# Two-layer diffusion backbone on one core: low parts, Y sums and squares of the projections pinned behind the VectorE work issued before them while a norm chain runs

## The chip, the core and the metric

The kernel runs on one core of one Trainium2 chip. TensorE (PE) multiplies, VectorE (DVE) and ScalarE (ACT) do the elementwise work, SyncE (SP) issues nearly all transfers, GpSimd (POOL) is unused. The metric is the device time of one execution in microseconds (us), the median of the runs; lower is better. One execution was also profiled, and all views are of that one. The trace gives the TensorE clock as a granted share: 1.0 is 2.4 GHz and 0.5 is 1.2 GHz.

## The reference, cut to what matters

There are 640 tokens (512 latent, 128 context) of width 1024, and two layers. Each layer is a feed-forward block, a token mixer (differential attention in layer 0, a gated linear recurrence, HGRN2, in layer 1) and another feed-forward block: six sub-layers in a row. Each of the six has a norm before and a norm after:

```python
def ada_pre(x, mod, j, g):
    return rmsnorm(x, g) * (1 + scale) + shift
def ada_post(x, y, mod, j, g, res_w):
    return x + res_w * gate * rmsnorm(y, g)
def ffn_sublayer(x, mod, j, g_pre, g_post, w_in, w_out):
    return ada_post(x, swiglu(ada_pre(x, mod, j, g_pre), w_in, w_out), mod, j, g_post, 0.5)
```

So between two sub-layers every token passes: sum of squares of the output Y, reciprocal root, X plus the scaled Y, sum of squares of X, reciprocal root, scaled X, which is the input H of the next projection.

## The kernel before, in words

Activations lie transposed: 128 features on the partitions, tokens along the row, eight blocks of 128 features. The 640 tokens are two groups of 320, g=0 and g=1.

**Projections.** A projection is a list of jobs; a job multiplies one 128-column unit of weights with H (or G, the hidden activations) for one group or both. Weights and activations are each split into a high and a low part: `convert` has ScalarE make the high part of a unit (L360) and puts the low part's subtraction on VectorE (L362) on a list, which `flush_lo` empties at the next unit or shortly after. Per feature block a job issues two matmuls with the high part (L452) and one with the low part (L457). The unit of a job is converted about three jobs ahead of it. Raw weights come through four buffers. The last projection of a sub-layer adds its parts into Y (L1132, VectorE, or a copy by ScalarE for a first part), and a square of Y (ScalarE, L555) is added to a sum `acc` (L556, VectorE). Four PSUM banks are taken in turn.

**Links.** `link` joins two sub-layers. The last eight jobs of the old one come once for g=0 and then for g=1. When g=0 is done, its norm chain (`chain_gen`) starts in the background beside the g=1 jobs; when g=1 is done, the second chain starts beside the first g=0 jobs of the next sub-layer (eight of a feed-forward block, five of attention, seven of HGRN), and it must be issued whole before that sub-layer's first g=1 job. A chain is, in order: three small matmuls that sum `acc` over partitions (L522), a reciprocal root by Newton steps on VectorE (L529, then L507 to L517), a matmul that spreads it over the partitions (L534), eight blocks of X plus scaled Y (L573, L579) with squares (L556), then again L522, L529 to L517 and L534, and eight blocks of scaled X, of which ScalarE makes the high part of H (L611) and VectorE the low part (L606 before, L619 after it). A step of a chain is issued at fixed places within the jobs (`step_bg`).

**Order.** What stands in the program in this order is the order of issue. A scheduler then fixes the order on each engine at compile time: of the instructions that its model of time holds to be ready, it takes the one issued first. So an instruction issued later can come ahead of one that is not yet ready, if nothing ties them. In the trace, each engine runs the order that was fixed.

The five links are called here A (feed-forward to attention), B (attention to feed-forward), C (feed-forward to feed-forward), D (feed-forward to HGRN) and E (HGRN to feed-forward). c0 and c1 are the chains of the two groups. J0, J1, ... are the first jobs of the sub-layer after a link; for a feed-forward block J0 to J7 are for g=0 and J8 on for g=1, where J8 and J9 use the weights of J6 and J7, and J10 and J11 those of J4 and J5, while J12 on load theirs again.

Of the kernel before, what the change touches and what calls it, by code (L numbers as in the profile page):

```python
# [14 lines left out]
ALU = mybir.AluOpType  # L15
# [203 lines left out]
class Net:  # L219
# [31 lines left out]
    def setup(self):  # L251
        tc, ctx = self.tc, self.ctx
        P = lambda n, b, **k: ctx.enter_context(tc.tile_pool(name=n, bufs=b, **k))
        self.const = P("const", 1)
        self.big = P("big", 1)
        self.rawp = P("rawp", RAW_BUFS)
        self.hlp = P("hlp", 1)
        self.hl = self.hlp.tile([128, 2, QUARTERS * 4, 128], F32R, name="whl")
        self.hl_next = 0
        self.los = []  # L260
        self.np_ = P("nrm", 3)
        self.small = P("small", 2)
        self.aux = P("aux", 2, space=PSUM)
        self.mm = P("mm", 1, space=PSUM)
        self.spill = P("spill", 1, space=bass.MemoryType.DRAM)
        self.lane = 0
        self.in_attn = False
        big = self.big
        self.Y = [big.tile([128, KT, NG], F32, name="Y0"), None]
        self.new_x()  # L270
        self.H = big.tile([128, 2, KT, NTOK], F32R, name="H")
        c = self.const
        self.ident = c.tile([128, 128], F32, name="ident")
        self.sel = c.tile([128, 3, 32], F32, name="sel")
        self.CV = c.tile([128, KT, 2], F32, name="CV")
        self.ones = c.tile([128, 1], F32, name="ones")
        self.MODF = c.tile([128, DEPTH * NMOD * KT, 2], F32, name="MOD")
        self.MOD = self.MODF.rearrange("p (l n) s -> p l n s", l=DEPTH)
        self.NGt = c.tile([128, 96], F32, name="NGt")
        self.BM = c.tile([128, 144], F32, name="BM")  # L280
        self.DT = c.tile([128, 50], F32, name="DT")
        self.PRE = c.tile([128, DEPTH, 3, KT, 2], F32, name="PRE")
        self.POST = c.tile([128, DEPTH, 3, KT, 2], F32, name="POST")
        self.acc = {}
        for g in range(2):
            self.acc[g] = c.tile([128, NG], F32, name=f"acc{g}")
        self.lam = c.tile([128, 1], F32, name="lam")
        self.lb = c.tile([128, 2, 16], F32, name="lb")
        self.again = c.tile([128, 1], F32, name="again")
# [35 lines left out]
    def place(self, u):  # L325
# [11 lines left out]
        u.w = [self.hl[:, r, 4 * a:4 * b, :] for r in range(2)]  # L337
        return True

    def flush_lo(self):  # L340
        for f in self.los:
            f()
        self.los.clear()

    def convert(self, n):
# [279 lines left out]

    def chain_gen(self, l, j, nxt, g, ready):
        ps = self.aux_tile()
        yield from self.post_gen(l, j, g, ps, nxt is not None)
        if nxt is not None:
            yield from self.pre_gen(nxt[0], nxt[1], g, ps, ready)  # L630
        else:
            yield from self.store_gen(g)

    def store_gen(self, g):
        nc = self.nc
        for tb in (0, 1, 2):
            n = min(NG - tb * 128, 128)
            ps = self.aux_tile()
            for kt in range(KT):
                nc.tensor.transpose(  # L640
                    ps[0:n, kt * 128:(kt + 1) * 128], self.X[:, kt, tb * 128:tb * 128 + n], self.ident
                )
            ob = self.fin_p.tile([128, 1024], F32, name="ob", tag="ob", bufs=2)
            nc.scalar.activation(out=ob[0:n, 0:512], in_=ps[0:n, 0:512], func=AF.Copy)
            nc.vector.tensor_copy(ob[0:n, 512:1024], ps[0:n, 512:1024])
            nc.sync.dma_start(out=self.o["y_sample"][0, tb * 128:tb * 128 + n, :], in_=ob[0:n, :])
            yield
# [478 lines left out]
    def y_part(self, f, ps, g, first, last):  # L1126
        nc = self.nc
        y = self.Y[g][:, f, :]
        if first:
            nc.scalar.activation(out=y, in_=ps, func=AF.Copy)  # L1130
        else:
            nc.vector.tensor_tensor(out=y, in0=y, in1=ps, op=ALU.add)  # L1132
        if last:
            while len(self.later) > 1:
                self.later.pop(0)()
            self.later.append(self.square(g, y, f == 0))

    def w_out_jobs(self, w, ready, cut):
        jobs = []
# [588 lines left out]
```

## Time and profile before

| | |
|---|---|
| time, median of 3 runs | 2783.96 us (2780.76 to 2785.59) |
| the profiled execution's own time | 2780.47 us |
| its span in the trace | 2778.7 us |
| mean granted TensorE clock | 0.99 |
| TensorE matmuls busy | 2715.6 us (98%) |
| VectorE busy | 1977.8 us (71%) |
| ScalarE busy | 1307.3 us (47%) |

The span goes from the first to the last instruction; 1.8 us of the execution's time lie outside it. Busy shares are means over stages with different limits. A line number is that of the kernel before.

### The profile page before, as it was taken

The page shows a single profiled execution, that of the slowest core. Times are in us where ns is not written, and L with a number is a line of the kernel's source. Part 1 is how long each engine was busy: PE and PEld are TensorE (multiplying, and loading weights), DVE is VectorE, ACT ScalarE, POOL GpSimd, SP SyncE. Part 2 cuts the span into 40 slices and gives each one's busy share as a digit, 9 for nine tenths or more (in the row PEclk, how much of TensorE's full clock was granted, in tenths as well). Part 3 has the DMA queues.
Part 4 walks back from the last instruction along what each step waited for, and adds up shares of the span by engine and source line. Part 5 has one row for each costly group of instructions (what it writes and reads, how often), then busy time and mean ns, then how long its engine had stood idle before and what let it go on. Part 6 is the DMA issues. An engine that isn't in the chain of part 4 may idle for free.

```text
span 2778.7 us, 47467 instructions
## 1 busy us (share of the span) xinstructions
PE 2715.6 (98%) x18670; PEld 2613.1 (94%) x18670; DVE 1977.8 (71%) x4285; ACT 1307.3 (47%) x2693; POOL 0.2 (0%) x4
## 2 busy tenths in 40 slices
PE   7999999899999999999999999999999999999998
PEld 5999999899998999999999999999999999999997
DVE  6766676887777965667786657687677678867574
ACT  4443444476675553435354434443343345545363
POOL 0000000000000000000000000000000000000000
PEclk9999999999999999999999999999999999999999
DMA  9556224211122456524244442421221222323231
GB/s 305 176 192 198 81 77 145 60 53 54 46 74 75 161 161 201 165 81 145 69 143 132 142 145 77 137 78 35 61 58 50 60 65 93 90 77 90 78 122 54
DMA packets 426077, 299.10 MB, mean 108 GB/s; under 512 B 9051, under 2 KB 386429, under 8 KB 424829
## 3 DMA queue, kind: packets, MB, share of 16 engines
q1 hardware_dynamic: 425344, 295.86, 34.6%
q8 instruction: 147, 2.41, 0.4%
q14 instruction: 78, 0.63, 0.1%
q10 hardware_dynamic: 508, 0.20, 0.0%
HBM read 280.82 MB, written 15.20 MB: 107 GB/s over the span
## 4 chain that ended last, share of the span: by engine, by line
PE 89%; DVE 5%; ACT 4%; DMA 1%; issue 1%; ACTq 0%; DVEq 0%; SPq 0%
PE mmps L484 31%; PE mmps L452 30%; PE mmps L457 15%; PE aux L1564 2%; PE aux L763 2%; PE mmps L1403 1%; DVE whl L362 1%; PE aux L1372 1%; ACT p L1302 1%; PE aux L1373 1%; PE aux L522 1%; PE aux L1601 1%; PE aux L534 1%; ACT whl L360 1%; ACT sq L1635 0%
## 5 line engine op out<-in xcount | busy, mean ns | idle before, releaser
L360 ACT ACTIVATE whl<-wraw 128x512 fp32r<-128x512 f32 (+4 forms) x644 | 464.2, 722 | 661.3 <-PE mmps L452 369.6
L362 DVE TENSOR_TENSOR whl<-wraw,whl 128x512 fp32r<-128x512 f32 (+4 forms) x644 | 515.3, 801 | 207.8 <-ACT whl L360 199.6
L452 PE MATMUL mmps<-H,whl 128*128 128x320 f32 x2624 | 571.5, 317 | 9.3 <-ACT H L611 6.9
L484 PE MATMUL mmps<-H,whl 128*128 128x320 f32 x3456 | 544.1, 309 | 0.1
L484 PEld LDWEIGHTS mmps<-H,whl 128*128 128x128 f32 x3456 | 515.3, 188 | 10.5 <-issue 4.2
L452 PE MATMUL mmps<-G,whl 128*128 128x320 f32 x2448 | 487.7, 311 | 3.8 <-ACT G L1649 1.5
L452 PEld LDWEIGHTS mmps<-H,whl 128*128 128x128 f32 x2624 | 432.5, 191 | 19.5 <-ACT H L611 8.3
L452 PEld LDWEIGHTS mmps<-G,whl 128*128 128x128 f32 x2448 | 391.2, 188 | 13.7 <-issue 5.9
L457 PE MATMUL mmps<-H,whl 128*128 128x320 f32 x1312 | 369.6, 314 | 0.7 <-DVE whl L362 0.7
L484 PE MATMUL mmps<-T,whl 128*128 128x320 f32 x2160 | 352.5, 309 | 0.0
L484 PEld LDWEIGHTS mmps<-T,whl 128*128 128x128 f32 x2160 | 325.4, 188 | 5.0 <-issue 2.5
L457 PE MATMUL mmps<-G,whl 128*128 128x320 f32 x1224 | 304.9, 310 | 0.0
L457 PEld LDWEIGHTS mmps<-H,whl 128*128 128x128 f32 x1312 | 239.1, 191 | 1.1 <-DVE whl L362 1.0
L457 PEld LDWEIGHTS mmps<-G,whl 128*128 128x128 f32 x1224 | 211.4, 188 | 0.0
L452 PE MATMUL mmps<-G,H 128*128 128x320 f32 x880 | 198.7, 312 | 0.1
L1132 DVE TENSOR_TENSOR Y<-Y,mmps 128x320 f32<-128x320 f32 x208 | 94.8, 482 | 127.8 <-PE mmps L457 127.6
L452 PEld LDWEIGHTS mmps<-G,H 128*128 128x128 f32 x880 | 147.8, 189 | 0.3 <-ACT Y L1130 0.3
L457 PE MATMUL mmps<-G,H 128*128 128x320 f32 x440 | 137.3, 312 | 0.0
L452 PE MATMUL mmps<-H,G 128*128 128x320 f32 x448 | 103.5, 312 | 0.0
L997 ACT ACTIVATE sa<-sa 128x320 f32<-128x320 f32 x144 | 67.9, 471 | 66.4 <-DVE sa L1000 65.5
L135 DVE TENSOR_TENSOR s<-wraw 128x512 f32<-128x512 f32 x72 | 49.7, 690 | 69.0 <-DMA wraw<-in_ffn_w_in 68.9
L556 DVE TENSOR_TENSOR acc<-acc,sq 128x320 f32<-128x320 f32 x168 | 80.1, 485 | 22.1 <-ACT sq L555 21.2
(260 smaller groups left out, 3572.5 us busy)
## 6 DMA issues: line engine op xcount, KB each, us to landing
wraw<-in_ffn_w_in SPq DMA_DIRECT2D x192, 512.0 KB, 4.3
wmod<-in_w_mod SPq DMA_DIRECT2D x66, 1024.0 KB, 7.1
wraw<-in_hgrn_w_in SPq DMA_DIRECT2D x40, 512.0 KB, 3.9
wraw<-in_ffn_w_out SPq DMA_DIRECT2D x32, 448.0 KB, 3.7
wraw<-in_ffn_w_out SPq DMA_DIRECT2D x32, 384.0 KB, 3.3
wraw<-in_attn_w_in SPq DMA_DIRECT2D x24, 512.0 KB, 3.8
xs<-X SPq DMA_DIRECT2D x4, 2560.0 KB, 12.8
wraw<-in_ffn_w_out SPq DMA_DIRECT2D x32, 320.0 KB, 3.2
```

Of the source, the lines that this page charges most:

```text
L135: V.tensor_tensor(out=z, in0=a[:, lo], in1=b[:, lo], op=ALU.subtract)
L360: nc.scalar.activation(out=u.w[0][:, 0:nk, :], in_=src, func=AF.Copy)
L362: self.los.append(lambda: nc.vector.tensor_tensor(out=u.w[1][:, 0:nk, :], in0=src, in1=u.w[0][:, 0:nk, :].bitcast(F32), op=ALU.subtract))
L452: nc.tensor.matmul(out=ps[g][:, 0:NG], lhsT=w[0][:, a, :], rhs=rhs[:, r, b, g * NG:(g + 1) * NG], start=(i == 0 and r == 0), stop=False,)
L457: nc.tensor.matmul(out=ps[g][:, 0:NG], lhsT=w[1][:, a, :], rhs=rhs[:, 0, b, g * NG:(g + 1) * NG], start=False, stop=(i == last),)
L484: nc.tensor.matmul(out=ps[:, 0:NG], lhsT=w[a][:, k, :], rhs=j.operand(r, k), start=(j.first and k == 0 and n == 0), stop=(k == 3 and n == ...
L522: self.nc.tensor.matmul(out=ps[:, c0 + n:c0 + n + 1], lhsT=acc[:, b0:b0 + 128], rhs=self.ones, start=True, stop=True,)
L556: return lambda: nc.vector.tensor_tensor(out=acc, in0=acc, in1=sq, op=ALU.add)
L763: self.nc.tensor.matmul(out=ps[g * 32:(g + 1) * 32, 0:512], lhsT=CS[:, k, 30 - 2 * i:62 - 2 * i], rhs=ts[half][:, g, :], start=first and h ...
L997: A.activation(out=e[name], in_=e[name], func=AF.Silu)
L1132: nc.vector.tensor_tensor(out=y, in0=y, in1=ps, op=ALU.add)
L1564: nc.tensor.matmul(out=ps[:, c * 128:(c + 1) * 128], lhsT=km[:, c * 128:(c + 1) * 128], rhs=self.view(Q2, c * 128, dims), start=True, stop ...
```

## The change

A counter `chains` holds how many chains are being issued. While it is above zero, the low parts, the later adds into Y, and the adds of Y's squares are each tied to the VectorE instruction issued just before them: `keep_in_program_order` records that the instruction may not stand ahead of that one in VectorE's order. It is a tie of order alone, without a semaphore. Instructions that are issued later are not tied, and neither are the chains' own instructions, the product of the gated hidden activations (L969, L972), or low parts that are issued after a chain has ended. No instruction is added or removed.

```diff
@@ setup
         self.los = []
+        self.chains = 0
@@
+    def behind(self, ins):
+
+        if self.chains:
+            self.tc.keep_in_program_order(ins)
+
     def flush_lo(self):
         for f in self.los:
-            f()
+            self.behind(f())
         self.los.clear()
@@ chain_gen
         ps = self.aux_tile()
+        self.chains += 1
         yield from self.post_gen(l, j, g, ps, nxt is not None)
         if nxt is not None:
             yield from self.pre_gen(nxt[0], nxt[1], g, ps, ready)
         else:
             yield from self.store_gen(g)
+        self.chains -= 1
@@ y_part
         else:
-            nc.vector.tensor_tensor(out=y, in0=y, in1=ps, op=ALU.add)
+            self.behind(nc.vector.tensor_tensor(out=y, in0=y, in1=ps, op=ALU.add))
         if last:
             while len(self.later) > 1:
                 self.later.pop(0)()
-            self.later.append(self.square(g, y, f == 0))
+            add = self.square(g, y, f == 0)
+            self.later.append(add if f == 0 else lambda: self.behind(add()))
```

## Rows read from the trace of the kernel before

**Rows 1.** Page, busy time of the engines: us, share of the span, instructions.

```profile
PE 2715.6 (98%) x18670; PEld 2613.1 (94%) x18670; DVE 1977.8 (71%) x4285; ACT 1307.3 (47%) x2693; POOL 0.2 (0%) x4
```

**Rows 2.** TensorE's waits: us in total, times, longest.

```profile
PE mmps L452 <- ACT H L611: 6.9, 6, 2.0
...
PE aux L534 <- DVE rs_y L517: 4.2, 4, 2.5
PE aux L522 <- DVE acc L556: 3.9, 2, 2.3
...
PE mmps L457 <- DVE whl L362: 0.7, 1, 0.7
```

**Rows 3.** Windows, five links summed: us, busy time of each engine.

```profile
sum 332.00, PE 315.82 PEld 305.14 DVE 296.08 ACT 161.89 POOL 0.00; mean PE 63.16 PEld 61.03 DVE 59.22 ACT 32.38 POOL 0.00
```

**Rows 4.** Timeline, VectorE, link E: start, us, instruction, idle before it.

```profile
2316.90 0.16 DVE L529 TENSOR_SCALAR rs_v<-aux 128x3 f32<-128x3 f32 x1 [0.53 <-PE aux L522]
...
2320.38 1.22 DVE L362 TENSOR_TENSOR G<-wraw,G 128x1024 fp32r<-128x1024 f32 x1
...
2323.73 1.23 DVE L362 TENSOR_TENSOR whl<-wraw,whl 128x1024 fp32r<-128x1024 f32 x1 [0.38 <-ACT whl L360]
...
2326.16 1.23 DVE L362 TENSOR_TENSOR whl<-wraw,whl 128x1024 fp32r<-128x1024 f32 x1 [0.47 <-ACT whl L360]
...
2337.54 0.48 DVE L556 TENSOR_TENSOR acc<-acc,sq 128x320 f32<-128x320 f32 x1
...
2344.66 0.15 DVE L517 SCALAR_TENSOR_TENSOR rs_y<-rs_a,rs_y 128x3 f32<-128x3 f32 x1
...
2352.58 0.67 DVE L619 SCALAR_TENSOR_TENSOR H<-nt,MOD,H 128x128 fp32r<-128x128 f32 x2
```

**Rows 5.** Timeline, TensorE, link E: first low-part matmuls of J5, J6, J7, J12.

```profile
2333.12 0.31 PE L457 MATMUL mmps<-H,G 128*128 128x320 f32 x1
...
2336.64 0.31 PE L457 MATMUL mmps<-H,whl 128*128 128x320 f32 x1
...
2340.84 0.30 PE L457 MATMUL mmps<-H,whl 128*128 128x320 f32 x1
...
2363.70 0.31 PE L457 MATMUL mmps<-H,whl 128*128 128x320 f32 x1
```

**Rows 6.** Timeline, link B: c1's last L517; first low-part matmuls of J6, J12.

```profile
920.77 0.16 DVE L517 SCALAR_TENSOR_TENSOR rs_y<-rs_a,rs_y 128x3 f32<-128x3 f32 x1
...
915.08 0.31 PE L457 MATMUL mmps<-H,whl 128*128 128x320 f32 x1
...
938.92 0.31 PE L457 MATMUL mmps<-H,whl 128*128 128x320 f32 x1
```

**Rows 7.** The same for link C.

```profile
1393.50 0.16 DVE L517 SCALAR_TENSOR_TENSOR rs_y<-rs_a,rs_y 128x3 f32<-128x3 f32 x1
...
1389.22 0.31 PE L457 MATMUL mmps<-H,whl 128*128 128x320 f32 x1
...
1412.18 0.31 PE L457 MATMUL mmps<-H,whl 128*128 128x320 f32 x1
```

**Rows 8.** Timeline, link A: a low part in c0's root; TensorE before J0.

```profile
509.30 1.22 DVE L362 TENSOR_TENSOR G<-wraw,G 128x1024 fp32r<-128x1024 f32 x1
...
511.14 0.80 PE L522 MATMUL aux<-ones,acc 128*128 128x1 f32 x6 [2.35 <-DVE rs_y L517]
511.80 0.86 PE L534 MATMUL aux<-ident,rs_y 128*128 128x128 f32 x6
513.90 0.90 PE L452 MATMUL mmps<-H,whl 128*128 128x320 f32 x2 [1.23 <-ACT H L611]
```

**Rows 9.** Windows, start of link C: busy (instructions), PEclk, DMA share, GB/s.

```profile
1361.00:1365.00 4.00, 4.00 (x21) 4.00 (x22) 3.15 (x13) 1.65 (x4) 0.00 (x0) 0.69 0.00 0
```

**Rows 10.** Timeline, VectorE, last link: a Y sum and the last L645.

```profile
2745.16 0.49 DVE L1132 TENSOR_TENSOR Y<-Y,mmps 128x320 f32<-128x320 f32 x1
...
2753.97 0.68 DVE L645 COPY ob<-aux 64x512 f32<-64x512 f32 x1 [0.60 <-ACT ob L644]
```

## The prediction

> **What bounds the kernel now.** I read the page first: TensorE's matmuls fill 2715.6 us of the 2778.7 us span [rows 1], so the time is TensorE's, and a change of order on VectorE counts only where TensorE waits for VectorE. Then TensorE's waits [rows 2]. The largest that the norm chains cause are those for H (6.9 us), for the root (4.2 us) and for the sum of squares (3.9 us): 15.0 us, 0.5% of the time. Low parts cost it 0.7 us: they come early enough now. The windows of the five links [rows 3] show who sets the pace there: VectorE is busy for 296.1 of 332 us, 89% against 71% over the span, while TensorE is busy for 315.8 and so idle for 16.2 us. In a link VectorE has nearly no time to spare, and what the change can move is who is served first.
>
> The timeline of VectorE in link E [rows 4] shows what order was fixed. c1's first root starts at 2316.90, and the low parts of J5, J6 and J7 (three, the first at 2320.38, the last at 2323.73) stand between its Newton steps. By the code these are issued much later: J5's behind an add of squares of c1 (the L556 at 2337.54), J6's behind the end of c1's second root (the L517 at 2344.66), J7's behind one of the last low parts of H (the first L619 of the pair at 2352.58). So VectorE runs them 17 to 29 us ahead of their place. TensorE wants them [rows 5] at 2333.12, 2336.64 and 2340.84. Each of these times lies *before* the instruction behind which the change ties the low part. That is the core of my argument.
>
> **The change part by part.** *Ties of low parts.* Nothing is added or removed, so the price is lateness. A low part holds VectorE for 1.2 us [rows 4]. In link E, J3's and J4's low parts ran early too, and get their places at the start of c1's body.
>
> J5: the L556 ends at 2338.0. Three low parts in front of it go behind it (-3.6), J3's comes in (+1.2): it ends at 2335.6 and the low part at 2336.8, 3.7 us after TensorE wants it.
>
> J6: the L517 ends at 2344.8. Two low parts (J6's, J7's) go behind it (-2.4) and J3's comes in (+1.2): 2343.6, and the low part is there at 2344.8 instead of 2336.64: 8.2 us late. This contains the first delay: J5, once started, needs the 3.5 us from one job to the next [rows 5].
>
> J7: the L619 ends at 2352.9, with J7's own 1.2 us out and J3's in, and the low part at 2354.1. J6 is through at 2344.8 + 3.5 = 2348.3. J7 cannot follow, but J8, J10 and J11 can: their weights (J6's, J4's, J5's) are there, and their H arrives from 2347 on, since before J7's low part come nearly all of c1's H. In before, the jobs for g=1 already run interleaved over four banks as H arrives. I let them fill the hole.
>
> Then J6 to J11, six jobs of 3.5 us and the 0.9 us of the spreading matmul [rows 8], run from 2344.8 to J12's low-part matmul at 2344.8 + 21.1 + 0.9 = 2366.8, against 2363.70 now: **+3.1 us in link E**. It is less than the 8.2 us of lateness, because TensorE waited for H behind J7 in any case.
>
> Links B and C enter the same feed-forward block of eight g=0 jobs. In B c1's second root ends at 920.9 [rows 6]; J6's and J7's low parts go out (-2.4), J3's and J4's, which ran before c1, come in (+2.4). J6's is there at 922.1 instead of 915.08, J12 at 922.1 + 22.0 = 944.1 against 938.92: **+5.2 us**. In C the root ends at 1393.7 [rows 7], of which J7's goes out (-1.2): J6's is there at 1393.7 instead of 1389.22, J12 at 1415.7 against 1412.18: **+3.5 us**.
>
> In link A the order works the other way. Low parts of J3 and J4 (one at 509.30) stand in c0's second root, and TensorE waits 2.35 + 1.23 us for that root and for H before J0 [rows 8]. With only five g=0 jobs, c1 is early enough in the order that these low parts come in time behind it. J0 starts 2.4 us sooner; but the two low parts then stand in c1, for which the first g=1 job waits, and give most of it back. I take **-1.4 us**, between 0 and the -3.6 of the whole wait. For D, with seven g=0 jobs and the same pattern, I take **-1.0 us** with the same ends.
>
> *Ties of Y sums and squares.* In A, C and D two Y sums per link, and adds of squares, go behind the last step of c0's second root, a few us later. I cost this at nothing: the bank that a Y sum frees is wanted four jobs later, and c1 starts with the last square, which is not earlier now. Without that cover it costs TensorE the same few us per link. In the last link a Y sum at 2745.16 is tied behind the last copy of outputs at 2753.97 [rows 10], 9 us later. Its bank is wanted four jobs on, some 16 us later, and the end hangs on the later Y sums: nothing; without cover, a few us.
>
> *DMA.* A raw buffer is free when its low part is made, so a late low part holds back the load four units on. J12's weights take J3's buffer; J3's low part now stands before J5's at 2336.8, and J12 is wanted at 2363.70: 27 us hide that load. If they did not, J12 would wait for it once per link.
>
> The sum: 3.1 + 5.2 + 3.5 - 1.4 - 1.0 = **+9.4 us**.
>
> The bounds: two low parts of later jobs (one at 2326.16 [rows 4]) are not tied and stand in c1 in B, C and E. If they drift out, each of these links gains 2.4: +2.8, +1.1, +0.7, and with -3.6 in A and D the sum is -2.6. At the other end the hole before J7 stays unfilled (2354.1 - 2348.3 = 5.8 us, three times 17.4), A and D give nothing (+2.4), and each feed-forward link gets a new stretch at the low clock: behind the 1.96 us wait at the start of link C the granted clock of 4 us was 0.69 [rows 9], that is 1.2 GHz for 2.5 of them; which doubles the time of 1.2 us of matmuls; as a bound I take that per link, 3.7 in all. That is 9.4 + 17.4 + 2.4 + 3.7 = +33.
>
> **The rivals.** *Faster: the chain is the bottleneck and wins.* The first root of c1 in E has 3.6 us of low parts between its steps; if c1 ends that much earlier in every link, and J5's to J7's low parts still come in time, most of the 15.0 us of waits [rows 2] goes: half of it, -7.5, gives 2776.5. For it speaks that the waits for the root and H are just where the low parts stand. Against it speak the three times of rows 5. It decides from the point where c1's second root ends before J6 wants its low part; in E it would have to end 8.2 us sooner.
>
> *Neutral: the same work in another order.* VectorE's work up to the last H is the same sum, and TensorE waits for that H in any case. If J5's and J6's stalls only take the place of waits for H, and A and D give what they can, the sum lies within 0.2%. The lower bound, -2.6, is this case: 2781.
>
> *Much slower: the hole stays unfilled.* The order of matmuls is fixed at compile time. If the model of time makes J7's low part come sooner than the chip does, J8's matmuls stand behind J7's. Then 17.4 us come on top, 2811. For it speaks that TensorE waits inside the interleaved jobs for single H blocks now; against it, that they are interleaved at all. By the Trainium skill ("TensorE: Matmul & The Clock Gate", The mechanism) matmuls start and end strictly in program order; by that rule nothing at run time fills the hole, and the time would be that of this rival if the compiled order does not. The trace agrees in that each link's jobs follow one fixed sequence.
>
> **How the numbers follow.** The profiled execution took 2780.47 us, 1.8 of them outside the span and 3.5 below the median of 2783.96. +9.4 gives 2789.9 on it, and 2793 on the median, which I forecast. A measurement of this kernel can tell about 0.2%, 5.6 us, from no change. Chances: the forecast case (+5.6 to +18) 0.45, unfilled holes 0.10, neutral 0.27, faster 0.18; so slower 0.55, same 0.27, faster 0.18. The range 2776 to 2806 goes on the fast side to about half of the faster rival and above to where the unfilled holes begin; for the forecast case alone it is 2789 to 2802.
>
> **What would show it.** In the changed trace c1's first root in link E should run without low parts of J5 to J7 between its steps and take about 4 us instead of 8 or more. The low parts of J5, J6 and J7 should follow L556, L517 and L619, and TensorE's waits for L362, 0.7 us now, should grow by 10 us or more, nearly all in B, C and E, while its waits for L517 and L611 shrink. J12's matmul in E should come some 3 us later, counted from the link's start; in A the wait before J0 should be about half. I am wrong if c1 ends more than 8 us sooner, if TensorE finds other work during J5 and J6, or if the scheduler, with its model of time, moves work outside the links.

## The result, and the profile after

| | before | after |
|---|---|---|
| time, median | 2783.05 us (4 runs, 2780.76 to 2785.59) | 2802.11 us (4 runs, 2796.96 to 2802.93) |
| the profiled execution | 2780.47 us, clock 0.990 | 2796.96 us, clock 0.990 |

The change makes the kernel slower: ratio 1.0069, 95% interval 1.0057 to 1.0082, which is 19 us. The direction and the range of the prediction (2793 us, 2776 to 2806) hold; the +9.4 us of its sum is half of what was measured. The profiled execution is the fastest of the four; the other three ran at a mean granted clock of 0.986 to 0.987. So its trace, 16.5 us above that of before at the same clock, shows a little less than the whole loss. In the code after the change the low part is L368, the H of ScalarE L617, the low part of H L625, the job's matmuls L458 and L463, the sums over partitions L528, the root L535 to L523, the spreading matmul L540, the add of squares L562, the two bodies L579 and L612, the Y sum L1140.

The page's engine line, and TensorE's waits (who waited <- for whom: us in total, times, longest):

```profile
PE 2719.1 (97%) x18670; PEld 2614.2 (94%) x18670; DVE 1984.7 (71%) x4285; ACT 1307.3 (47%) x2693; POOL 0.2 (0%) x4
```

```profile
PE aux L528 <- DVE acc L562: 7.8, 5, 2.6
...
PE aux L540 <- DVE rs_y L523: 6.4, 3, 3.6
PE mmps L463 <- DVE G L368: 5.6, 4, 1.8
...
PE mmps L458 <- ACT H L617: 4.6, 6, 1.3
...
PE mmps L458 <- DVE Y L1140: 2.0, 3, 0.7
...
PE mmps L463 <- DVE whl L368: 1.2, 3, 0.7
```

And one row of before that [rows 2] does not have:

```profile
PE aux L522 <- DVE rs_y L517: 2.3, 1, 2.3
```

Against [rows 1] no engine has noticeably more work: TensorE +3.5 us, VectorE +6.9 us. The span grows by 16.5 us, so 13.0 us of it are idle time of TensorE. The waits for low parts go from 0.9 us (0.7 for whl in [rows 2] and 0.2 for G) to 6.8 us, since the low parts lie in either tile; that is as predicted in kind. But the waits for the chain do not shrink in return. Those for H fall from 8.6 us (6.9 for ScalarE's part, 1.7 for VectorE's) to 5.3 (4.6 and 0.7), those for the root stay (4.2 and 2.3 before, 6.4 after), and those for the sum of squares double (3.9 to 7.8): 19.0 us before, 19.5 after. Without low parts in its way the chain was to become faster, and TensorE waits for it as long as before. Three waits for tied Y sums, 2.0 us in all, are new.

Where it was lost is seen from how much later the same matmul comes in the changed trace, ahead of each link and behind it (us, profiled executions):

| link | A | B | C | D | E | sum |
|---|---|---|---|---|---|---|
| predicted | -1.4 | +5.2 | +3.5 | -1.0 | +3.1 | +9.4 |
| measured | +0.5 | +2.0 | +7.8 | +3.5 | +3.3 | +17.1 |

One trace tells a link only to some 3 us: in the experiments below, links in which every engine runs the order of before came out between -0.6 and +3.3 us.

**Link E, for which the numbers were worked out, ran as predicted.** VectorE in E, timeline (start, us, instruction, idle before it); E's chain starts 13.1 us later in this trace:

```profile
2330.12 0.16 DVE L535 TENSOR_SCALAR rs_v<-aux 128x3 f32<-128x3 f32 x1 [0.60 <-PE aux L528]
...
2333.36 0.16 DVE L523 SCALAR_TENSOR_TENSOR rs_y<-rs_a,rs_y 128x3 f32<-128x3 f32 x1
...
2336.08 1.22 DVE L368 TENSOR_TENSOR whl<-wraw,whl 128x1024 fp32r<-128x1024 f32 x1
2337.21 1.22 DVE L368 TENSOR_TENSOR G<-wraw,G 128x1024 fp32r<-128x1024 f32 x1
...
2349.07 1.22 DVE L368 TENSOR_TENSOR G<-wraw,G 128x1024 fp32r<-128x1024 f32 x1
...
2357.57 0.15 DVE L523 SCALAR_TENSOR_TENSOR rs_y<-rs_a,rs_y 128x3 f32<-128x3 f32 x1
2357.64 1.22 DVE L368 TENSOR_TENSOR whl<-wraw,whl 128x1024 fp32r<-128x1024 f32 x1
...
2365.82 1.22 DVE L368 TENSOR_TENSOR whl<-wraw,whl 128x1024 fp32r<-128x1024 f32 x1
```

And TensorE, first low-part matmuls of J5, J6, J7 and J12, which answer to [rows 5]:

```profile
2350.35 0.42 PE L463 MATMUL mmps<-H,G 128*128 128x320 f32 x1 [1.79 <-DVE G L368]
...
2358.91 0.41 PE L463 MATMUL mmps<-H,whl 128*128 128x320 f32 x1 [0.25 <-DVE whl L368]
...
2367.37 0.31 PE L463 MATMUL mmps<-H,whl 128*128 128x320 f32 x1
...
2380.13 0.31 PE L463 MATMUL mmps<-H,whl 128*128 128x320 f32 x1
```

c1's first root is free of J5's to J7's low parts and takes 3.4 us (2330.12 to 2333.52). J3's and J4's now follow it in c1's body. The last three come as tied, J6's directly behind the end of c1's second root. Less 13.1 us, the low parts end at 2337.2, 2345.8 and 2353.9 (predicted 2336.8, 2344.8, 2354.1), and J12's matmul starts at 2367.0 (predicted 2366.8).

**Link C is where it was worse.** VectorE in C, from c0's first root to c1's last H (windows: length, then busy time of PE, PEld, DVE, ACT, POOL, granted clock, DMA share, GB/s), the sum line being that over all five links; first before, then after:

```profile
1333.78:1404.32 70.54, 68.58 (x453) 64.39 (x453) 62.03 (x185) 32.85 (x65) 0.00 (x0) 0.98 0.41 127
...
sum 337.42, PE 321.24 PEld 310.56 DVE 301.22 ACT 165.31 POOL 0.00; mean PE 64.25 PEld 62.11 DVE 60.24 ACT 33.06 POOL 0.00
```

```profile
1336.74:1413.49 76.75, 70.82 (x448) 65.04 (x448) 63.56 (x185) 32.48 (x65) 0.00 (x0) 0.93 0.37 121
...
sum 350.22, PE 321.80 PEld 305.45 DVE 305.10 ACT 164.35 POOL 0.00; mean PE 64.36 PEld 61.09 DVE 61.02 ACT 32.87 POOL 0.00
```

The chains of C take 6.2 us longer, those of all links 12.8. In C both stretches hold 185 VectorE instructions, with 1.5 us more of work; the other 4.7 us are idle time of VectorE. Over all five links it is 3.9 us of work and 8.9 us of idle time (36.2 to 45.1 us). Seen from TensorE, C's 6.2 us are 4.0 us more of idle time (2.0 to 5.9) and 2.2 us more of matmul time, and the 12.8 us of all links are nearly all idle time (16.2 to 28.4). Three waits of VectorE beside c1 in C show it, before and then after:

```profile
1370.96 1.26 DVE L573 SCALAR_TENSOR_TENSOR nt<-Y,POST,aux 128x192 f32<-128x192 f32 x4 [0.89 <-PE aux L534]
...
1386.53 0.16 DVE L529 TENSOR_SCALAR rs_v<-aux 128x3 f32<-128x3 f32 x1 [0.41 <-PE aux L522]
...
1389.42 0.49 DVE L969 TENSOR_TENSOR gm<-sa,mmps 128x320 f32<-128x320 f32 x1 [0.52 <-PE mmps L457]
```

```profile
1375.93 1.26 DVE L579 SCALAR_TENSOR_TENSOR nt<-Y,POST,aux 128x192 f32<-128x192 f32 x4 [2.62 <-PE aux L540]
...
1394.33 0.16 DVE L535 TENSOR_SCALAR rs_v<-aux 128x3 f32<-128x3 f32 x1 [1.46 <-PE aux L528]
...
1399.44 0.49 DVE L977 TENSOR_TENSOR gm<-sa,mmps 128x320 f32<-128x320 f32 x1 [2.41 <-PE mmps L463]
```

VectorE waits 6.5 us here instead of 1.8, each time for TensorE, and the tied low parts do not run in these gaps. TensorE in turn waits for a low part in the same place, and runs at half clock behind that wait (timeline, then windows):

```profile
1392.12 0.56 PE L463 MATMUL mmps<-H,G 128*128 128x320 f32 x1 [1.78 <-DVE G L368]
```

```profile
1392.20:1399.00 6.80, 6.80 (x27) 6.80 (x28) 3.23 (x12) 0.47 (x1) 0.00 (x0) 0.50 0.94 294
```

In before TensorE neither waits nor slows down in this part of C (window):

```profile
1380.00:1404.00 24.00, 24.00 (x157) 20.29 (x156) 21.66 (x63) 10.69 (x26) 0.00 (x0) 1.00 0.87 285
```

Half of 6.8 us is 3.4 us: by this estimate up to 3.4 of C's +7.8 us are the clock's.

### The profile page after: what moved, and what is told of

Its sections match the earlier page's. It is cut to its first block, busy times and chain, and to the rows that moved or that the text cites. A ratio compares the mean times of both kernels' runs of the same rounds, so it can differ in the third digit from the quotient of the medians.

```text
span 2795.2 us, 47452 instructions
## 1 busy us (share of the span) xinstructions
PE 2719.1 (97%) x18670; PEld 2614.2 (94%) x18670; DVE 1984.7 (71%) x4285; ACT 1307.3 (47%) x2693; POOL 0.2 (0%) x4
## 4 chain that ended last, share of the span: by engine, by line
PE 85%; DVE 8%; ACT 4%; DMA 2%; issue 1%; ACTq 0%; DVEq 0%; SPq 0%
PE mmps L490 31%; PE mmps L458 28%; PE mmps L463 14%; PE aux L1573 2%; PE aux L771 2%; DVE whl L368 1%; PE mmps L1412 1%; PE aux L1381 1%; DVE acc L562 1%; ACT p L1311 1%; DMA wraw<-in_ffn_w_out 1%; PE aux L528 1%; PE aux L1382 1%; PE aux L540 1%; PE aux L1610 1%
## 5 line engine op out<-in xcount | busy, mean ns | idle before, releaser
L368 DVE TENSOR_TENSOR whl<-wraw,whl 128x512 fp32r<-128x512 f32 (+4 forms) x644 | 516.3, 803 | 197.8 <-ACT whl L366 189.9
L458 PE MATMUL mmps<-H,whl 128*128 128x320 f32 x2624 | 567.3, 316 | 6.6 <-ACT H L617 4.6
L458 PE MATMUL mmps<-G,whl 128*128 128x320 f32 x2448 | 487.6, 312 | 4.2 <-ACT G L1658 1.2
L458 PEld LDWEIGHTS mmps<-H,whl 128*128 128x128 f32 x2624 | 430.3, 190 | 14.1 <-ACT H L617 6.2
L458 PEld LDWEIGHTS mmps<-G,whl 128*128 128x128 f32 x2448 | 391.0, 188 | 14.3 <-issue 5.9
L463 PE MATMUL mmps<-H,whl 128*128 128x320 f32 x1312 | 368.9, 314 | 1.2 <-DVE whl L368 1.2
L463 PE MATMUL mmps<-G,whl 128*128 128x320 f32 x1224 | 305.4, 310 | 0.0
L463 PEld LDWEIGHTS mmps<-H,whl 128*128 128x128 f32 x1312 | 238.3, 190 | 2.7 <-DVE whl L368 1.8
L463 PEld LDWEIGHTS mmps<-G,whl 128*128 128x128 f32 x1224 | 211.5, 188 | 0.0
L458 PE MATMUL mmps<-G,H 128*128 128x320 f32 x880 | 199.4, 313 | 0.0
L1140 DVE TENSOR_TENSOR Y<-Y,mmps 128x320 f32<-128x320 f32 x208 | 95.0, 484 | 128.0 <-PE mmps L463 127.8
L458 PEld LDWEIGHTS mmps<-G,H 128*128 128x128 f32 x880 | 147.7, 188 | 0.0
L463 PE MATMUL mmps<-G,H 128*128 128x320 f32 x440 | 136.7, 311 | 0.0
L458 PE MATMUL mmps<-H,G 128*128 128x320 f32 x448 | 104.6, 320 | 4.1 <-DVE gm L977 2.7
L562 DVE TENSOR_TENSOR acc<-acc,sq 128x320 f32<-128x320 f32 x168 | 80.7, 489 | 24.4 <-ACT sq L561 22.8
```

The costliest lines, as they stand in the source:

```text
L368: self.los.append(lambda: nc.vector.tensor_tensor(out=u.w[1][:, 0:nk, :], in0=src, in1=u.w[0][:, 0:nk, :].bitcast(F32), op=ALU.subtract))
L458: nc.tensor.matmul(out=ps[g][:, 0:NG], lhsT=w[0][:, a, :], rhs=rhs[:, r, b, g * NG:(g + 1) * NG], start=(i == 0 and r == 0), stop=False,)
L463: nc.tensor.matmul(out=ps[g][:, 0:NG], lhsT=w[1][:, a, :], rhs=rhs[:, 0, b, g * NG:(g + 1) * NG], start=False, stop=(i == last),)
L562: return lambda: nc.vector.tensor_tensor(out=acc, in0=acc, in1=sq, op=ALU.add)
L1140: self.behind(nc.vector.tensor_tensor(out=y, in0=y, in1=ps, op=ALU.add))
```

## The experiments

Each is the changed kernel with the edit shown; only ties differ, no work is left out. Microseconds are the ratio's distance from one times 2782 us, about the median of before in these runs.

**Theory.** At first, theory L: the loss is the lateness of J5's to J7's low parts. Rivals: the Y sums and squares (Y), or work of chain c0.

**e1: low parts alone.** Y sums and squares are free.

```diff
-            self.behind(nc.vector.tensor_tensor(out=y, in0=y, in1=ps, op=ALU.add))
+            nc.vector.tensor_tensor(out=y, in0=y, in1=ps, op=ALU.add)
...
-            self.later.append(add if f == 0 else lambda: self.behind(add()))
+            self.later.append(add)
```

> Only the low parts are tied, Y sums and squares are as before the change. Theory L (the cost is the lateness of the low parts of the last jobs for g=0, which stand behind chain c1): nearly the whole loss stays, +14 to +20 us against the kernel before, with the first job for g=1 weights of their own (J12) late by 2 to 4 us in link E as in the whole change. Rival Y (the ties of Y sums and squares hold back banks and the sum that c1 starts with): the loss falls to +6 us or less.

Measured 2798.53 us, ratio 1.0051 (1.0034 to 1.0068): 14 us. The low parts carry most of it, and rival Y falls.

**e2: Y sums and squares alone.**

```diff
     def flush_lo(self):
         for f in self.los:
-            self.behind(f())
+            f()
```

> Only Y sums and squares are tied, low parts are free. Theory L: no loss, within 4 us of the kernel before in either direction. Rival Y: +10 us or more. Rival S (any tie makes the scheduler fix another order all over, and the loss is that of a less lucky order): +5 us or more, in places that have nothing to do with the ties.

Measured 2788.40 us, ratio 1.0020 (1.0010 to 1.0029): 5.6 us, more than theory L expected and less than Y. It has the size of rival S, but not its places: in the trace all of it lies in A (+3.4) and D (+5.0), where sums are tied; B, C and E are at -1.0, 0.0 and -0.6. What the tied sums do there is seen in A. c1's first root, before and then e2, and TensorE's wait for the sum of squares ahead of c1's second root in e2:

```profile
512.12 0.15 DVE L529 TENSOR_SCALAR rs_v<-aux 128x3 f32<-128x3 f32 x1
```

```profile
514.41 0.16 DVE L535 TENSOR_SCALAR rs_v<-aux 128x3 f32<-128x3 f32 x1 [0.55 <-PE aux L528]
```

```profile
534.62 0.37 PE L528 MATMUL aux<-ones,acc 128*128 128x1 f32 x1 [7.22 <-DVE acc L562]
```

Counted from c0's first root (484.29 and 481.87) c1 starts after 27.8 us before and after 32.5 us in e2: 4.7 us later, since the last add of squares of Y, which c1 starts with, now stands among c0's last steps.

**e3: ties only once c1 has started.**

```diff
-        if self.chains:
+        if self.second:
             self.tc.keep_in_program_order(ins)
...
+        self.second += g
         yield from self.post_gen(l, j, g, ps, nxt is not None)
...
+        self.second -= g
```

> All ties, but only from the start of the second chain c1; what is issued beside c0 alone is free. Theory L: the loss stays, +12 to +20 us, since the late low parts are all issued beside c1. Rival F (the ties beside the first chain c0 cost it, by pushing low parts of J0 to J2 and Y sums behind c0's second root and so J0's start): +5 us or less.

Measured 2793.83 us, ratio 1.0045 (1.0030 to 1.0060): 12.5 us, as theory L expected; rival F, that the ties beside c0 are the cost, falls as the main cause. The ties beside c1 carry about two thirds.

**e4: the low parts of J5 to J7 of each feed-forward block free, the rest tied.**

```diff
+        for j in jobs[-3:]:
+            j.unit.free = True
...
-        for f in self.los:
-            self.behind(f())
+        for f, free in self.los:
+            i = f()
+            if not free:
+                self.behind(i)
```

> The whole change, but the low parts of the last three jobs for g=0 of each feed-forward block (J5, J6, J7 in links B, C, E) are free. Theory L: links B, C and E cost nothing, what is left is link D's +3 us and at most 3 us elsewhere: 0 to +6 us in all. Rivals Y, F and S: +10 us or more stays.

Measured 2792.86 us, ratio 1.0039 (1.0024 to 1.0054): 10.9 us are left. Theory L expected at most 6 and falls: the lateness of these three is not the whole. What is left is what the other low parts (J3's and J4's among them), the sums and the two mixer links cost, which the next runs separate in part. Beside L stands from here on theory P, the pace of the chains: c1 does not end sooner, since the moved work stands in front of it. Rival S is from here on the chance of single runs.

**e5 and e6: all ties, but only in links A and D, or only in B, C and E.**

```diff
-        self.chains += 1
+        tie = nxt is not None and nxt[1] == 1
+        self.chains += tie
...
-        self.chains -= 1
+        self.chains -= tie
```

(For e6 the condition is `nxt[1] != 1`.)

> All ties of the change, but only in links A and D (into attention and into HGRN); B, C, E and the last link are as before. My prediction's own terms for the two links: -1.4 and -1.0, so about 2.4 us faster. Theory P (what c0's second root gains, the moved low parts and Y sums take back in front of c1's body; TensorE starts J0 earlier and then waits in one longer stretch before the first g=1 job, with more time at 1.2 GHz): slower by 4 to 8 us, A and D about half each. Rival S (what A and D lost in the traces so far is the chance of single runs): within 2 us of before.

> All ties of the change, but only in the three links into feed-forward blocks (B, C, E). Theory L (late low parts of J5 to J7 plus a later end of c1): slower by 10 to 14 us, most of it in C. If links add up, this and the run with A and D alone give together the 19 us of the whole change, within 4 us; if one link's order depends on another's, they do not. Rival: A and D carry most of the loss, then this one is slower by less than 8 us.

Measured e5 2789.98 us, ratio 1.0025 (1.0014 to 1.0036), 7.0 us; e6 2793.85 us, ratio 1.0049 (1.0037 to 1.0062), 13.6 us. Together they give 20.6 us of 19, so links add up within the intervals. e5 lies where theory P had it, e6 where theory L had it once a later end of c1 was added to L. My terms had A and D as a gain of 2.4 us. TensorE in A shows what became of it: first before, ahead of the first g=1 job (the waits ahead of J0 are in [rows 8]), then e5, ahead of both; its trace stands 2.4 us ahead of before at the start of A:

```profile
538.23 0.88 PE L534 MATMUL aux<-ident,rs_y 128*128 128x128 f32 x6 [2.49 <-DVE rs_y L517]
540.39 0.90 PE L452 MATMUL mmps<-H,whl 128*128 128x320 f32 x2 [1.28 <-ACT H L611]
```

```profile
508.73 0.38 PE L458 MATMUL mmps<-H,G 128*128 128x320 f32 x1 [0.68 <-DVE Y L1141]
510.12 0.80 PE L528 MATMUL aux<-ones,acc 128*128 128x1 f32 x6 [1.00 <-DVE acc L562]
512.58 0.90 PE L458 MATMUL mmps<-H,whl 128*128 128x320 f32 x2 [1.26 <-ACT H L617]
534.49 0.83 PE L528 MATMUL aux<-ones,acc 128*128 128x1 f32 x6 [2.56 <-DVE acc L562]
539.17 1.54 PE L540 MATMUL aux<-ident,rs_y 128*128 128x128 f32 x6 [3.85 <-DVE rs_y L523]
541.99 0.90 PE L458 MATMUL mmps<-H,whl 128*128 128x320 f32 x2 [1.29 <-ACT H L617]
```

Ahead of J0 the waits shrink from 3.58 us [rows 8] to 2.94; ahead of the first g=1 job they grow from 3.77 to 7.70. And c0's second root ends earlier (VectorE's timeline, before and e5):

```profile
510.91 0.15 DVE L517 SCALAR_TENSOR_TENSOR rs_y<-rs_a,rs_y 128x3 f32<-128x3 f32 x1
```

```profile
500.30 0.16 DVE L523 SCALAR_TENSOR_TENSOR rs_y<-rs_a,rs_y 128x3 f32<-128x3 f32 x1
```

Counted from c0's first root (484.29 and 481.89) that is 26.6 and 18.4 us: 8.2 us sooner. But c1 ends 4.0 us later in A (68.0 for 64.0 us, to the start of its last H) and 3.1 us later in D, counted in the same way. TensorE is through J0 to J4 0.8 us sooner and waits for c1 longer. The rows above show where c1 loses its 4.0 us in A. With the 2.4 us added, its first sum (510.12) comes 1.4 us later than before (511.14 [rows 8]), behind a wait for the tied squares; the spread of its second root (539.17) 3.3 us later; and its H (541.99) 4.0 us later. Between the Newton steps of this second root now stands a low part (VectorE, e5); before, no low part ran in A from 512.2 us, where c1 starts, to 551.0:

```profile
536.06 1.21 DVE L368 TENSOR_TENSOR whl<-wraw,whl 128x1024 fp32r<-128x1024 f32 x1
```

Over the two links together, between the same matmuls (windows; before, then e5):

```profile
sum 173.83, PE 161.62 PEld 157.67 DVE 154.49 ACT 85.24 POOL 0.00; mean PE 80.81 PEld 78.83 DVE 77.24 ACT 42.62 POOL 0.00
```

```profile
sum 180.15, PE 162.94 PEld 157.86 DVE 156.79 ACT 84.97 POOL 0.00; mean PE 81.47 PEld 78.93 DVE 78.39 ACT 42.49 POOL 0.00
```

6.3 us longer: 5.0 of them idle time of TensorE (12.2 to 17.2), 1.3 slower matmuls.

**e7: the opposite of e4, only J5's to J7's low parts tied.** (`if free` for `if not free`, sums free.)

> The opposite of freeing the last three: of everything that the change ties only the low parts of J5, J6 and J7 of each feed-forward block keep their tie; other low parts, Y sums and squares are as before. Theory L (lateness of these three is the main cost): slower by 6 to 11 us, all of it in B, C and E, with stalls of TensorE on low parts there, and A and D unchanged. Theory P (the pace of the chain, set by the other tied work, is the main cost): slower by less than 3 us, and c1 ends earlier than before, since J5 to J7's low parts no longer stand in it.

Measured 2785.70 us, ratio 1.0009 (1.0000 to 1.0018): 2.5 us. Theory L falls for good: their lateness by itself costs at most 5 us (the interval's end). As P expected, c1 ends a little sooner than before, by 0.8 us in B, 0.1 in C and 1.9 in E, counted from c0's first root. In E the trace shows why (TensorE, first low-part matmuls of J6, J7, J12; line numbers are six higher, and this trace stands 5.3 us behind before at the start of E):

```profile
2348.20 0.41 PE L469 MATMUL mmps<-H,whl 128*128 128x320 f32 x1 [0.25 <-DVE whl L374]
...
2356.65 0.31 PE L469 MATMUL mmps<-H,whl 128*128 128x320 f32 x1
...
2369.41 0.31 PE L469 MATMUL mmps<-H,whl 128*128 128x320 f32 x1
```

J7's matmul is 10.5 us late (2356.65 - 5.3 - 2340.84), J12's 0.4: g=1 jobs run in the hole, and nearly the whole lateness is given back. In the changed kernel J7's is 13.4 us late and J12's 3.3 [rows 5]: 2.9 us more, and all 2.9 arrive at J12. In both traces J12 comes 12.76 us behind J7, against 22.86 before, so 10.1 us of lateness are covered and every further one counts. The cover is not all g=1 work: 87 matmuls of jobs stand between the two where 119 stood, and the spread of c1's second root, 2.3 us of waits and 3.4 us at half clock (2349.0 to 2352.4), which before had in this stretch, are not in it. That is one link and one trace each.

**e8: Y sums and squares alone, and only in B, C and E** (e2 and the condition of e6).

> Only the Y sums and the adds of squares are tied, and only in links B, C and E, where the run with these ties alone lost nothing (its trace stood 1.0, 0.0 and 0.7 us ahead of before there). If those gains are real and the links independent: faster by 1 to 2 us. Rival S (chance of single runs): within 1 us either way. Slower by more than 3 us would say that the schedule of one link depends on ties in another.

Measured 2778.69 us, ratio 0.9994 (0.9985 to 1.0003): 1.7 us faster by the ratio, inconclusive by its interval. With e2 it follows, if links add up, that the sums cost A and D about 7 us (5.6 + 1.7; the last link, which e2 ties too, shows nothing in the traces), as much as all ties together do there.

**Theory M.** From e4 to e7: J3's and J4's low parts, which before ran while c0 waited, are tied into the start of c1's body. They delay c1, and with it J5 to J7, past the cover. Rival R: any low part kept out of the chains' idle time costs the same.

**e9 and e10: J3's and J4's low parts free and the rest tied; or these two alone tied.** e4 and e7 with `jobs[-5:-3]` for `jobs[-3:]`.

> The whole change, but the low parts of J3 and J4 of each feed-forward block are free. Theory M (in B, C and E the loss is mostly that J3's and J4's low parts, which ran while c0 waited, are tied into the start of c1's body, where they delay c1 and with it J5 to J7): B, C and E lose no more than the run with the last three alone, 1 to 4 us together, and with 7 us from A and D the whole is slower by 8 to 11 us. Rival R (any low part held out of the chains' idle time costs the same, J3 and J4 are nothing special): slower by 14 us or more.

> Only the low parts of J3 and J4 of each feed-forward block keep their tie. Theory M: c1's body starts and ends later in B, C and E while J5 to J7 still run inside it, so c1 ends 1 to 3 us later in each of these links; slower by 3 to 8 us. Rival R: two of some eight tied pieces of work per link, slower by less than 3 us.

Measured e9 2792.21 us, ratio 1.0040 (1.0027 to 1.0052), 11.1 us, of which 7.0 are A and D (e5); e10 2785.95 us, ratio 1.0012 (1.0003 to 1.0021), 3.3 us. e9 lies at the upper end of what theory M expected (8 to 11) and e10 at its lower end, so M is not refuted; but rival R is not excluded either, since its 14 us for e9 lies just inside the interval (7.5 to 14.5) and its less than 3 us for e10 as well (0.8 to 5.8). In C the premise of M holds for J3's low part alone: J4's, the first in G, stood in c1's body already in before, 35.1 us after c0's first root (now 41.9). By time alone J3 and J4 are nothing special: with them free 11.1 us are left, with J5 to J7 free 10.9. The chains' length in C, windows of e9, of e10, of e7, and of e5, where nothing in C is tied:

```profile
1339.09:1409.40 70.31, 66.87 (x435) 60.87 (x435) 63.12 (x185) 32.70 (x65) 0.00 (x0) 0.98 0.40 129
```

```profile
1332.56:1406.71 74.15, 72.06 (x459) 65.84 (x459) 62.39 (x185) 32.78 (x65) 0.00 (x0) 0.95 0.41 135
```

```profile
1333.27:1403.74 70.47, 67.84 (x435) 62.40 (x435) 61.08 (x184) 32.51 (x65) 0.00 (x0) 0.95 0.36 120
```

```profile
1335.17:1407.29 72.12, 70.16 (x453) 65.97 (x453) 62.07 (x185) 32.85 (x65) 0.00 (x0) 0.95 0.39 124
```

Before it is 70.54 us, with the whole change 76.75. J3 and J4 alone make it 74.15, J5 to J7 alone 70.47, all but J3 and J4 70.31. The order of before itself gives 70.54 to 72.12 (e5), so J3's and J4's low parts alone stretch C's chains by 2.0 to 3.6 us, and the whole change by 4.6 to 6.2. Theory M had c1 end 1 to 3 us later in each of the three links with these two alone: it is 3.3 us in B (70.70 for 67.38), and nothing in E (68.23 for 68.42).

**e11: ties only while c0 runs alone.** (`if self.chains and not self.second`, with e3's counter.)

> Ties only while c0 runs alone; once c1 has started nothing is tied. With the ties beside c1 alone the kernel was 11 us slower, so if the two halves add up this one is slower by 8 us, most of it in A and D (7 us, where the ties act on c0's second root). Theory M expects less in B, C and E than there is in A and D: slower by 5 to 9 us in all. The prediction's own terms for c0 (a gain of 2.4 us in A and D) expect it not slower.

Measured 2787.10 us, ratio 1.0017 (1.0009 to 1.0026): 4.7 us, just below the 5 to 9 that theory M expected; clearly not the gain of my terms. With e3's 12.5 us that is 17.2 of 19.

**e12: e8, and in link B also J5's to J7's low parts tied.**

```diff
-        for f in self.los:
-            self.behind(f())
+        for f, free in self.los:
+            i = f()
+            if free and self.in_b:
+                self.behind(i)
...
+        tie = nxt is not None and nxt[1] != 1
+        b = nxt is not None and tuple(nxt) == (0, 2)
+        self.chains += tie
+        self.in_b += b
```

> The run with the sums tied in B, C and E, and in link B also the low parts of J5 to J7, since B was the one link that the last three alone did not delay (its trace stood 1.2 us ahead there). If both gains are real and add up: faster than before by 3 to 5 us. Rival S (the gains are chance of single runs): between 3 us faster, as with the sums alone, and no change. Slower than before would say that the last three cost B something once the sums are tied.

Measured 2777.47 us against 2781.72 (11 and 29 runs), ratio 0.9984 (0.9976 to 0.9993): 4.5 us faster than before, the one version that is clearly faster than both kernels. It is less than the 0.2% that I took as told from no change, but the interval excludes one. Rival S's 3 us lie inside the interval too, and which of its two parts gives the gain is not settled: in its trace B gains 0.4 and E 2.0 us, and another 2.9 us lie ahead of the first link, where no tie acts.

Links in the traces of the experiments that tell them apart (us against before, worked out as above; one trace each):

| | A | B | C | D | E | by the ratio |
|---|---|---|---|---|---|---|
| all ties in A and D (e5) | +3.3 | -0.6 | +2.5 | +3.8 | 0.0 | +7.0 |
| all ties in B, C, E (e6) | +0.2 | +2.5 | +8.1 | -0.1 | +3.2 | +13.6 |
| J5 to J7 alone (e7) | 0.0 | 0.0 | +3.5 | +3.1 | +0.4 | +2.5 |
| all but J3, J4 (e9) | +3.7 | +0.8 | +2.9 | +3.4 | +0.2 | +11.1 |
| J3, J4 alone (e10) | -0.1 | +0.1 | +3.5 | +3.3 | 0.0 | +3.3 |

In B, C and E the pairs do not add up: 2.5 (e7) and 3.3 (e10) stand against 13.6 (e6). Without J3 and J4 4.1 us remain (11.1 - 7.0), without J5 to J7 3.9 (10.9 - 7.0). My reading is that either alone stays mostly within the cover and both together exceed it; E shows it in numbers, B and C do not. No run ties J3 to J7 and nothing else: e6 also ties the low parts of earlier jobs. From the differences above (4.1 = x + 2.5 - 1.7, and 3.9 = x + 3.3 - 1.7) I estimate these at 2 to 3 us, so that some 7 of the 13.6 us come only from the ties together.

## Why the prediction was right, and where its sizes were off

The direction is right because tied low parts do cost TensorE more than the chains gain (e1, 14 us). That the time lies in the range is in part luck: the range reaches from the faster rival to the unfilled holes, 2802.11 us lies just beyond the 2789 to 2802 of the forecast case alone, and a term that is too large (B) makes up for a part of those that are too small.

**Lateness of J5 to J7 behind c1's steps: right.** In E three times came within 1 us, and the term (+3.1) is +3.3. In B J6's low-part matmul was 7.2 us late (predicted 7.0) and J12's 4.6 (predicted 5.2).

**The holes are filled: right.** TensorE runs g=1 jobs while J7 is late (e7: 10.5 us late, 0.4 remain). The order had been compiled with g=1 jobs ahead of J7's low-part matmuls, so the rival at 2811 did not come. The rule that I had weighed is that matmuls run strictly in program order (the Trainium skill, "TensorE: Matmul & The Clock Gate", The mechanism). The traces agree: in B, C and E of e5, where nothing is tied, the matmuls come one by one in the order of before.

**B, +5.2: too large by what lay behind J12.** I followed the loss only to J12. Small matmuls of the modulation (L763 before, L771 after) that stood behind J12 were compiled into the hole. Their windows in B, ahead of J12 and behind it; before, then after (length, busy time and number of these matmuls, clock):

```profile
891.00:938.92 47.92, 1.05 (x2) 1.00 0.36 119
...
938.92:962.00 23.08, 3.84 (x30) 1.00 0.72 233
```

```profile
893.00:942.99 49.99, 2.96 (x16) 1.00 0.53 169
...
942.99:964.00 21.01, 1.92 (x16) 1.00 0.46 151
```

1.92 us of work moved ahead of J12: 4.6 us at J12 (4.0, counted as in the table of links) become 2.0 behind it.

**C, +3.5: the largest mis-sized term (+7.8).** I had let J7's low part go out of c1 (-1.2) and nothing come in, though in B I had counted J3's and J4's (+2.4). In C these two stretch the chains by 2.0 to 3.6 us alone (e10), and all ties by 4.6 to 6.2. A term of 1.2 us per low part is too small in any case: of the 6.2 us only 1.5 are VectorE's work; 4.7 are idle time of VectorE, the largest pieces of it waits for TensorE, which was itself late and for 6.8 us at half clock.

**A and D, -1.4 and -1.0: the step that failed.** I had J0's earlier start as a gain of which c1 gives most back, with the ends 0 and -3.6. c0's root was indeed freed, by more than I took (8.2 us in A), but c1 ended 4.0 and 3.1 us later and TensorE's idle time grew by 5.0 us: +7.0 us (e5), outside my ends. The Y sums and squares that I cost at nothing are enough for it: e2 and e8 put them at about 7 us in A and D. I had written that c1 starts with the last square, "which is not earlier now"; it is later, by 4.7 us in A in e2. And the bank of a Y sum was not always free in time: TensorE waits 2.0 us for Y sums in the changed kernel and 0.7 us ahead of J0 in e5. My note that without cover they cost "the same few us per link" is what came. Low parts alone (e1) also lost 3.5 and 1.9 us there in one trace, the 1.9 within the scatter, so the two seem not to add up; which of them acts first in the whole change is not told apart.

**Signs to look for.** c1's first root in E ran free of J5's to J7's low parts and took 3.4 us, as I had said. The wait before J0 in A fell from 3.58 us to 1.92 (0.69 for a Y sum, 0.94 for c1's squares, 0.29 for H), about half as I had said, but for other causes. The waits for low parts grew by 5.9 us, not by 10 or more; those for H shrank; those for the root stayed (6.5 to 6.4), where I had said they shrink. My 15.0 us of waits for the chain had left out the rows of 2.3 us (root) and 1.7 us (VectorE's part of H): it was 19.0. The rival by which the chain wins needed c1's second root 8.2 us sooner in E; it came 0.2 us sooner (2357.57 - 13.1 against 2344.66 [rows 4]).

**What stays open.** Why VectorE and TensorE wait for each other longer in C is shown as a loop (late low part, late matmul, half clock, late spread), not taken apart. The clock's part in C, up to 3.4 us, is an estimate that no run tried. The low parts of the jobs before J3 were never tied alone, and J3's to J7's never without the rest.

## What to carry to other kernels

Where two engines are both nearly full in a stretch, as here, work that is off the chain need not be in the chain's way, since it can run in the chain's own gaps: tying it to its place in the program opened the first chain in A (8.2 us) and sent the bill to the next one. Price such a tie at the *last* consumer, through every chain that follows, and not at the step that it frees. And a delay with other work behind it cost next to nothing up to the length of that work and everything beyond it (10.1 us in E), so two nearly harmless ties (2.5 and 3.3 us) can be part of 13.6 us with their neighbours; tie one class in one link at a time, and keep what measures as a gain.

## What the runs showed of the hardware

The same program at the same order ran at a mean granted clock between 0.986 and 0.990, and its times went with it: 2796.96 us at 0.990, 2801.90 to 2802.93 us at 0.986 to 0.987. The kernel before did the same within 0.988 to 0.992 in the 65 executions of it beside the experiments: at 0.992 its mean time was 2778.4 us (3 runs), at 0.989 2783.2 us (21 runs). In C two waits of TensorE close together, 0.98 us and 1.78 us, were followed by 6.8 us at 0.50, that is 1.2 GHz, all of it with TensorE busy.
